# A transpose on one core: TensorE's program as a loop over three row chunks, PSUM in two halves, and copies that cover several ranges

## The chip, the core and the metric

The kernel runs on one core of a Trainium2 chip. The metric is the time on the device in microseconds (us) of one execution. The time before is 1265.63 us, the median of 8 runs (1265.09 to 1266.03).

## What is computed

```python
def setup_inputs():
    return {"x": np.random.randn(8192, 8192).astype(np.float32)}

def reference(x):
    return np.transpose(x)
```

The input and the output are float32, 268.44 MB each. The input is read once from HBM, and the output is written once.

## The kernel before

The input has 8192 rows and 8192 columns. The work is cut into 128 chunks: two halves of 4096 columns (`s`), each with 64 groups of 128 rows (`c`), first all of `s` = 0, then all of `s` = 1. The list `chunks` holds them in this order, and the loop over `t` (from 0 to 127) is written out in full when the program is made: every engine gets straight code, with no loop in it.

For each chunk one DMA loads 128 rows x 4096 columns (2 MB, 16 KB on each of 128 partitions) into one of three input buffers `ins[t % 3]` (line 99). TensorE turns the chunk in 32 transposes of 128 x 128 (line 139). Each transpose takes every fourth column of a block of 512 columns, so four transposes (`b`) make one block `q`, and a chunk has eight blocks. A block goes into one of eight PSUM tensors of 128 x 512, one for each bank. Even blocks are copied out by ScalarE (line 150) and odd ones by VectorE (line 152), each with one copy of 128 x 512.

The copies go into nine region buffers of 16 KB on each partition. A region collects one block `q` over up to eight chunks, so that its store writes long rows: a full region holds 1024 output columns, and its store moves 2 MB. The dictionary `window` says which region a block is collecting in, since which chunk. The blocks are out of step with one another: in chunk `t` one block's region is complete and closes (`q` = `c` mod 8), and in the next chunk that block opens a new region, taken from the list `free`. At the seam, between `s` = 0 and `s` = 1, a region holds the last groups of the one half and the first of the other, and two smaller stores empty it. The regions at the very start and at the very end are smaller too. There are 128 loads and 142 stores.

What sets the order around the change:

- SP (SyncE) issues all DMAs, into one queue, in the order in which the code writes them. First come the loads of chunks 0 to 2. Then for each chunk `t` come the stores of the blocks that close in it (line 172 for the first store, line 28 for all others), each behind a wait for its copy, and after them the load of chunk `t` + 3 behind a wait for TensorE's last transpose of chunk `t`.
- Within a chunk TensorE takes the blocks in the order `(c + k) % 8`, so the block that closes comes first, and the block that opens a new region comes last. It waits for the load of the chunk and, for each block, for the copy that empties its bank.
- A copy waits for TensorE. The copy that opens a region also waits until all stores from that region have landed (the semaphore `s_st` of the region, line 127).

The program's source is printed with its line numbers here.

Of the kernel before, what the change touches and what calls it, by code (L numbers as in the profile page):

```python
# [24 lines left out]
def wide_dma(nc, eng, queue, out, in_):  # L25


    return eng.add_instruction(
        mybir.InstDMACopy(
            mode="Copy",  # L30
            name=nc.get_next_instruction_name(),
            engine=eng.engine,
            ins=[physical(in_)],
            outs=[physical(out)],
            queue=queue,
        )
    )


@with_exitstack  # L40
def kernel(
    ctx: ExitStack,
    tc: tile.TileContext,
    x: bass.AP,
    out: bass.AP,
):

    nc = tc.nc
    P = 128
    N, M = x.shape
    assert x.shape == out.shape[::-1]
    dt = x.dtype

    S = 32
    B = 4  # L60
    W = 8
    NR = S // B
    NIN = 3
    NREG = 9
    NPS = 8
    CH = N // P
    J = S * P

    with tc.tile_critical():  # L69
        nc.alloc_sbuf_tensor("pad", [P, 32], dt)  # L70
        ident = nc.alloc_sbuf_tensor("ident", [P, P], dt).ap()
        ins = [nc.alloc_sbuf_tensor(f"in{k}", [P, J], dt).ap() for k in range(NIN)]
        regs = [nc.alloc_sbuf_tensor(f"reg{k}", [P, B * W * P], dt).ap() for k in range(NREG)]
        pss = [nc.alloc_psum_tensor(f"ps{k}", [P, B * P], dt).ap() for k in range(NPS)]

        s_id = nc.alloc_semaphore("s_id")
        s_ld = [nc.alloc_semaphore(f"s_ld{k}") for k in range(NIN)]
        s_st = [nc.alloc_semaphore(f"s_st{k}") for k in range(NREG)]
        s_pe = nc.alloc_semaphore("s_pe")
        s_cp = [nc.alloc_semaphore("s_cpa"), nc.alloc_semaphore("s_cpv")]  # L80

        nc.gpsimd.memset(ident, 0.0).then_inc(s_id, 1)  # L82
        nc.gpsimd.wait_ge(s_id, 1)
        nc.gpsimd.affine_select(  # L84
            out=ident,
            in_=ident,
            compare_op=mybir.AluOpType.not_equal,
            fill=1.0,
            base=0,
            pattern=[[-1, P]],  # L90
            channel_multiplier=1,
        ).then_inc(s_id, 1)
        nc.tensor.wait_ge(s_id, 2)

        chunks = [(s, c) for s in range(M // J) for c in range(CH)]

        def load(t):
            s, c = chunks[t]
            nc.sync.dma_start(
                out=ins[t % NIN], in_=x[c * P:(c + 1) * P, s * J:(s + 1) * J]  # L100
            ).then_inc(s_ld[t % NIN], 16)

        for t in range(NIN):
            load(t)

        n = 0
        copied = [0, 0]
        bank = [None] * NPS
        free = list(range(NREG))
        stored = [0] * NREG  # L110
        window = {}
        stores = 0
        for t, (s, c) in enumerate(chunks):
            nc.tensor.wait_ge(s_ld[t % NIN], 16 * (t // NIN + 1))
            closing = []
            for q in [(c + k) % NR for k in range(NR)]:
                if q not in window:


                    span = (q - c) % W + 1  # L120
                    r = free.pop(0)
                    parts = [(s, c, min(c + span, CH))]
                    if c + span > CH and t + span < len(chunks):
                        parts.append((s + 1, 0, c + span - CH))
                    window[q] = (t, r, parts)
                    if stored[r]:
                        (nc.scalar, nc.vector)[q % 2].wait_ge(s_st[r], 16 * stored[r])
                t0, r, parts = window[q]
                k = [p[0] for p in parts].index(s)
                base = B * P * sum(z - a for _, a, z in parts[:k])  # L130
                _, a, z = parts[k]
                rows = (z - a) * P
                view = regs[r][:, base:base + B * rows].rearrange("p (b i) -> p b i", b=B)
                ps = pss[n % NPS]
                e = q % 2
                if bank[n % NPS] is not None:
                    nc.tensor.wait_ge(*bank[n % NPS])
                for b in range(B):
                    last = nc.tensor.transpose(  # L139
                        ps[:, b * P:(b + 1) * P],  # L140
                        ins[t % NIN][:, q * B * P + b:(q + 1) * B * P - B + b + 1:B],
                        ident,
                    )
                last.then_inc(s_pe, 1)
                n += 1
                o = view[:, :, (c - a) * P:(c - a + 1) * P]
                i = ps.rearrange("p (b i) -> p b i", b=B)
                (nc.scalar, nc.vector)[e].wait_ge(s_pe, n)  # L148
                if e == 0:
                    cp = nc.scalar.copy(out=o, in_=i)  # L150
                else:
                    cp = nc.vector.tensor_copy(out=o, in_=i)  # L152
                cp.then_inc(s_cp[e], 1)
                copied[e] += 1
                bank[(n - 1) % NPS] = (s_cp[e], copied[e])
                if t + 1 == t0 + sum(z - a for _, a, z in parts):
                    closing.append((q, e, copied[e]))
            for q, e, count in closing:
                t0, r, parts = window.pop(q)
                nc.sync.wait_ge(s_cp[e], count)  # L160
                base = 0
                for s_, a, z in parts:
                    rows = (z - a) * P
                    j0 = s_ * J + q * B * P
                    dst = out[j0:j0 + B * P, a * P:a * P + rows]
                    dst = dst.rearrange("(q b) i -> q b i", q=P)
                    src = regs[r][:, base:base + B * rows]
                    base += B * rows
                    if stores:
                        st = wide_dma(nc, nc.sync, "qSPDynamicHW", dst, src)  # L170
                    else:
                        st = nc.sync.dma_start(
                            out=dst, in_=src.rearrange("q (b i) -> q b i", b=B)
                        )
                    st.then_inc(s_st[r], 16)
                    stores += 1
                    stored[r] += 1
                free.append(r)
            if t + NIN < len(chunks):
                nc.sync.wait_ge(s_pe, n)  # L180
                load(t + NIN)
        for r in range(NREG):
            nc.sync.wait_ge(s_st[r], 16 * stored[r])

# [29 lines left out]
```

## Time and profile before

| what | value |
|---|---|
| median of 8 runs | 1265.63 us |
| the profiled execution | 1265.43 us |
| its span | 1263.7 us |
| TensorE matmul busy | 746.2 us (59%), 4096 instructions |
| TensorE weight load busy | 722.3 us (57%), 4096 instructions |
| VectorE busy | 354.1 us (28%), 512 instructions |
| ScalarE busy | 300.9 us (24%), 513 instructions |
| data that the DMA queues moved | 537.51 MB, mean 425 GB/s |
| a load, median from issue to landing | 23.6 us |
| a store of 2 MB, median from issue to landing | 22.6 us |

The span runs from the first to the last record of the program in one profiled execution; the execution's own time is 1.7 us longer. "Busy" is the time in which an engine works on an instruction, and waits are not in it. The profile also cuts the span into 40 equal slices and gives for each the busy share of the DMA engines in tenths and what they moved in GB/s. There are 16 DMA engines on the core, and each DMA's rows are spread over all of them. A DMA queue's row gives its packets, the bytes in MB and the time of its packets as a share of the 16 engines' span: q1 is the queue of the loads and stores, and the queues marked "instruction" bring the engines' own programs. In a group of instructions the line of the kernel and the engine come first, then busy time and the mean time of one in ns, then the idle time before the group and what ended most of it. PE is TensorE, PEld its weight loads, DVE VectorE, ACT ScalarE, and SPq the queue in which SP issues DMAs.

### The profile page before, as it was taken

To read this page: it belongs to the slowest core of one execution; us is meant where nothing else is said; L and a number is where in the kernel's file an instruction comes from. 1 tells how busy PE (TensorE), PEld (TensorE's weight loads), DVE (VectorE), ACT (ScalarE), POOL (GpSimd) and SP (SyncE) were. 2 spreads that over 40 slices of the span, in tenths; PEclk is the share of its full clock that TensorE was granted. 3 is DMA by queue.
4 is the path that set the end of the run, shared out by engine and by line. 5 is a ranking of instruction groups with operands and counts; after the bars stand their busy time and mean duration, and the time that the engine had idled before them with its cause. 6 is when DMAs were issued, how large, how long until landed. Compare 5 with 4: busy or idle time off the path is not lost.

```text
span 1263.7 us, 9807 instructions
## 1 busy us (share of the span) xinstructions
PE 746.2 (59%) x4096; PEld 722.3 (57%) x4096; DVE 354.1 (28%) x512; ACT 300.9 (24%) x513; POOL 0.7 (0%) x6
## 2 busy tenths in 40 slices
PE   6656656565566655656556656666566665656561
PEld 6655556564566555655555655665556655656561
DVE  3322322322223222232222322223222232232220
ACT  3322222222222222222222222222222222222220
POOL 0000000000000000000000000000000000000000
PEclk9887786868767777676886786767777778686865
DMA  9999999999999999999999999999999999999998
GB/s 379 430 428 428 429 430 426 430 430 428 429 428 429 429 427 430 430 429 428 429 425 415 430 429 428 429 429 429 428 428 430 429 428 429 429 429 429 429 427 353
DMA packets 39308, 537.51 MB, mean 425 GB/s; under 512 B 4320, under 2 KB 4832, under 8 KB 6240
## 3 DMA queue, kind: packets, MB, share of 16 engines
q1 hardware_dynamic: 39264, 536.89, 99.9%
q8 instruction: 32, 0.52, 0.2%
q14 instruction: 12, 0.10, 0.0%
HBM read 268.44 MB, written 268.44 MB: 425 GB/s over the span
## 4 chain that ended last, share of the span: by engine, by line
DMA 78%; PE 19%; issue 0%; ACT 0%; SPq 0%; ACTq 0%
DMA in<-in_x_dram 78%; PE ps L139 19%; ACT reg L150 0%; SPq L209 0%; ACTq L148 0%; SPq L69 0%
## 5 line engine op out<-in xcount | busy, mean ns | idle before, releaser
L139 PE MATMUL ps<-ident,in 128*128 128x128 f32 x4096 | 746.2, 365 | 490.5 <-DMA in<-in_x_dram 490.5
L139 PEld LDWEIGHTS ps<-ident,in 128*128 128x128 f32 x4096 | 722.3, 220 | 514.2 <-DMA in<-in_x_dram 505.7
L152 DVE COPY reg<-ps 128x512 f32<-128x512 f32 x512 | 354.1, 692 | 882.8 <-PE ps L139 881.4
L150 ACT COPY reg<-ps 128x512 f32<-128x512 f32 x512 | 299.6, 585 | 935.6 <-PE ps L139 932.9
L150 ACT ACT_TABLE_LOAD x1 | 1.3, 1283 | 0.9 <-SPq L69 0.9
L84 POOL TENSOR_SCALAR_AFFINE_SELECT ident<-ident 128x128 f32<-128x128 f32 x1 | 0.3, 292 | 0.2 <-POOL ident L82 0.2
L82 POOL MEMSET ident<- 128x128 f32 x1 | 0.2, 204 | 0.5 <-SPq L69 0.5
L198 POOL MEMSET const-bfloat16-1.0<- 128x1 bf16 x1 | 0.1, 101 | 0.0
L198 POOL MEMSET const-uint8-127<- 128x1 uint8 x1 | 0.1, 101 | 0.0
L198 POOL MEMSET const-float32-0.0<- 128x1 f32 x1 | 0.1, 98 | 0.2 <-issue 0.2
L198 POOL MEMSET const-float32-1.0<- 128x1 f32 x1 | 0.1, 98 | 0.0
## 6 DMA issues: line engine op xcount, KB each, us to landing
in<-in_x_dram SPq DMA_DIRECT2D x128, 2048.0 KB, 23.6
out_dram<-reg SPq DMA_DIRECT2D x114, 2048.0 KB, 22.6
out_dram<-reg SPq DMA_DIRECT2D x4, 1792.0 KB, 19.8
out_dram<-reg SPq DMA_DIRECT2D x4, 1536.0 KB, 19.8
out_dram<-reg SPq DMA_DIRECT2D x4, 1280.0 KB, 19.6
out_dram<-reg SPq DMA_DIRECT2D x4, 1024.0 KB, 19.5
out_dram<-reg SPq DMA_DIRECT2D x4, 768.0 KB, 18.1
out_dram<-reg SPq DMA_DIRECT2D x4, 512.0 KB, 16.5
```

Of the source, the lines that this page charges most:

```text
L82: nc.gpsimd.memset(ident, 0.0).then_inc(s_id, 1)
L84: nc.gpsimd.affine_select(out=ident, in_=ident, compare_op=mybir.AluOpType.not_equal, fill=1.0, base=0, pattern=[[-1, P]], channel_multipl ...
L139: last = nc.tensor.transpose(ps[:, b * P:(b + 1) * P], ins[t % NIN][:, q * B * P + b:(q + 1) * B * P - B + b + 1:B], ident,)
L150: cp = nc.scalar.copy(out=o, in_=i)
L152: cp = nc.vector.tensor_copy(out=o, in_=i)
L198: nc = _bacc.Bacc("TRN2", target_bir_lowering=False, num_devices=1)
```

## The change

The changed kernel moves the same data in the same DMAs, with the same chunks, the same regions and the same buffers for the input. Five things are different.

1. **TensorE's program is a loop.** The function `transposes(t)` writes out one chunk. Chunks 0 and 1 are written out; the other 126 are 42 turns of a hardware loop with three chunks in it (one for each input buffer). A loop can't wait for rising counts, so TensorE takes back what it waited for: it waits until a load's semaphore is 16 and subtracts 16, and it waits until a half of PSUM is free (`s_bank`) and subtracts 1.
2. **PSUM is in two halves.** Each half is one tensor of 128 x 2048 and holds four blocks. TensorE always takes blocks 0 to 3 into the first half and 4 to 7 into the second, and signals after 16 transposes instead of after 4. ScalarE empties the first half, VectorE the second.
3. **One copy for several blocks.** All regions are one tensor `regs`. Where the places of neighbouring blocks in it lie a fixed distance apart and have the same row length, one copy takes up to four blocks. Where a block of the half closes, the four are cut into at least two copies, and the one with the closing block goes first.
4. **The wait for a region's earlier store** stands ahead of all copies of the half in which a region opens.
5. **The order on SP**: in each chunk the load of chunk `t` + 3 comes first and the stores after it. Among the stores of one chunk, the region that was opened first goes first.

The core of the diff (`SIZE` is the elements of a region on a partition, `NH` is 4, `T` is 128):

```diff
-        regs = [nc.alloc_sbuf_tensor(f"reg{k}", [P, B * W * P], dt).ap() for k in range(NREG)]
-        pss = [nc.alloc_psum_tensor(f"ps{k}", [P, B * P], dt).ap() for k in range(NPS)]
+        regs = nc.alloc_sbuf_tensor("regs", [P, NREG * B * W * P], dt).ap()
+        pss = [nc.alloc_psum_tensor(f"ps{h}", [P, NH * B * P], dt).ap() for h in range(2)]
...
+        def transposes(t):
+            k = t % NIN
+            nc.tensor.sem_inc(s_ld[k], -16).wait_op(s_ld[k], 16, "sem-ge")
+            for h in range(2):
+                if t:
+                    nc.tensor.sem_inc(s_bank[h], -1).wait_op(s_bank[h], 1, "sem-ge")
+                for b in range(NH * B):
+                    j = (h * NH + b // B) * B * P + b % B
+                    tr = nc.tensor.transpose(
+                        pss[h][:, b * P:(b + 1) * P],
+                        ins[k][:, j:j + B * P - B + 1:B],
+                        ident,
+                    )
+                tr.then_inc(s_pe, 1)
+
+        T = len(chunks)
+        nc.tensor.wait_ge(s_id, 2)
+        for t in range(T % NIN):
+            transposes(t)
+        with nc.Fori(0, T // NIN, engines=[nc.tensor.engine]):
+            for t in range(NIN):
+                transposes(T % NIN + t)
...
-            for q in [(c + k) % NR for k in range(NR)]:
...
-                (nc.scalar, nc.vector)[e].wait_ge(s_pe, n)
...
+            for h in range(2):
+                eng = (nc.scalar, nc.vector)[h]
...
+                        if stored[r]:
+                            eng.wait_ge(s_st[r], 16 * stored[r])
...
+                ends = [closes(window[h * NH + g], t) for g in range(NH)]
+                if any(ends) and len(runs) == 1:
+                    runs = [runs[0][:NH // 2], runs[0][NH // 2:]]
+                runs.sort(key=lambda u: not any(ends[g] for g in u))
+                eng.wait_ge(s_pe, 2 * t + h + 1)
+                for u in runs:
+                    off, dist = place[u[0]]
+                    dims = [list(regs.ap[0]), [dist, B], [1, P]]
+                    if len(u) > 1:
+                        dims.insert(1, [place[u[1]][0] - off, len(u)])
+                    o = bass.AP(regs.tensor, regs.offset + off, dims)
...
+                    if any(ends[g] for g in u):
+                        cp.then_inc(s_cp[h], 1)
...
+                        if u is runs[-1]:
+                            eng.wait_ge(s_cp[h], copied[h])
+                            eng.sem_inc(s_bank[h], 1)
+                    elif u is runs[-1]:
+                        cp.then_inc(s_bank[h], 1)
+            if t + NIN < T:
+                nc.sync.wait_ge(s_pe, 2 * t + 2)
+                load(t + NIN)
+            closing.sort(key=lambda k: window[k[0]][0])
...
-            if t + NIN < len(chunks):
-                nc.sync.wait_ge(s_pe, n)
-                load(t + NIN)
```

## The prediction, made before the changed kernel ran

> **What bounds the kernel now.** I read the page first, from the DMA rows up.
>
> ```profile
> DMA  9999999999999999999999999999999999999998
> GB/s 379 430 428 428 429 430 426 430 430 428 429 428 429 429 427 430 430 429 428 429 425 415 430 429 428 429 429 429 428 428 430 429 428 429 429 429 429 429 427 353
> ...
> q1 hardware_dynamic: 39264, 536.89, 99.9%
> q8 instruction: 32, 0.52, 0.2%
> q14 instruction: 12, 0.10, 0.0%
> ...
> L139 PE MATMUL ps<-ident,in 128*128 128x128 f32 x4096 | 746.2, 365 | 490.5 <-DMA in<-in_x_dram 490.5
> L139 PEld LDWEIGHTS ps<-ident,in 128*128 128x128 f32 x4096 | 722.3, 220 | 514.2 <-DMA in<-in_x_dram 505.7
> L152 DVE COPY reg<-ps 128x512 f32<-128x512 f32 x512 | 354.1, 692 | 882.8 <-PE ps L139 881.4
> L150 ACT COPY reg<-ps 128x512 f32<-128x512 f32 x512 | 299.6, 585 | 935.6 <-PE ps L139 932.9
> ```
>
> All 16 DMA engines are busy in every slice, at about 429 GB/s. TensorE is busy 59% of the span, VectorE 28%, ScalarE 24%, and each idles for the one before it. The queue alone bounds the kernel: 536.87 MB at 429 GB/s are 1251.4 us of the span of 1263.7. The change moves no byte of q1, so only the other 12.3 us can be won, and anything on the engines is free until a transfer is issued late. The two low slices are the start (first packet after 2 us, slow first packets) and the end (353 GB/s). The end is what I looked into.
>
> Each DMA reports its landing 16 times in the trace, once for each DMA engine. I took, for some loads and the last store, the 16 landing times, sorted, in us behind the first of the 16:
>
> ```
> load 0    0 .02 .02 .05 .08 .14 .16 .25 .26 .29 .30 .31 .33 .44 .48 .54
> load 30   0 .06 .19 .28 .30 .39 .56 .93 1.01 1.67 1.71 1.83 1.83 2.22 2.75 3.03
> load 63   0 .06 .29 .55 .86 1.04 1.07 1.92 3.01 3.05 3.21 3.22 3.31 3.69 4.25 4.42
> load 126  0 .11 .42 .66 1.45 2.42 2.66 4.13 6.27 6.44 6.50 6.69 6.78 7.11 7.39 7.46
> ```
>
> The engines drift apart, in steps. A step of 1.3 to 1.6 us (3.03 to 4.42, 2.22 to 3.69) follows each of the 32 fetches of q8, and always on one engine. Those 16 KB fetches come after every 248 to 266 TensorE instructions (16 KB / 256 = 64 B each): they load TensorE's own program. Eight engines end 6.3 to 7.5 us behind and the other eight 0 to 4.1: 32 fetches in turn on eight engines are four each, 4 x 1.45 = 5.8 us. The 12 fetches of q14 (8 KB; by the instruction counts ScalarE 5, VectorE 5, SyncE 2) make smaller steps, up to 1 us. Every DMA has its rows split over the engines in a fixed way, so no engine takes work from a late one, and the kernel ends with the latest.
>
> **Step 1: TensorE's loop (no fetches).** 42 turns over three chunks leave 128 + 192 of 8192 transpose instructions in the program. A turn is 96 x 2 + 9 semaphore instructions + 2 for the loop = 203, some 13 KB, less than one fetched block. If it stays in the engine, the eight lose four steps: 7.5 - 5.8 = 1.7 us behind at most. Then the other eight are the latest, at 4.13. No row shows a backward branch, so I bound its price: none to three blocks fetched a turn. Three is the case in which the body lies across a block boundary (the first crossing comes after some 220 to 240 of the instructions that the trace shows; the body takes places 138 to 341, so it does) and only two blocks are held: the first block again, the second again, and the one after it ahead of need. I take none, because the q8 fetches go round eight engines before they repeat, which looks to me like eight places for blocks, of which the loop uses two. That is an inference, not a row.
>
> [...]
>
> **Step 2: fewer copies.** The changed program holds 264 ScalarE and 259 VectorE copies instead of 512 each; with the semaphore instructions 330 and 324 instead of 577 and 576. At 128 instructions to 8 KB that is three fetches each instead of five: 12 become 8. The latest of the non-TensorE engines was hit by about three of the 12; it loses none to two steps of 1 us: 4.1 becomes 2.1 to 4.1, middle 3.1. Sum of steps 1 and 2: 7.5 - 3.1 = 4.4 us earlier (3.3 to 5.4). The copies themselves: four at 692 ns are 2.8 us at most for a half, inside a chunk's 9.76 us (three loads land 29.28 us apart). That a merged one is cheaper gains nothing, since both engines wait over 880 us for TensorE.
>
> **Step 3: the order on SP, and the store wait.** Now:
>
> ```profile
> SPq L99 <- PE ps L139: 465.9, 125, 8.8
> SPq L28 <- DVE reg L152: 321.2, 63, 9.3
> SPq L28 <- ACT reg L150: 311.1, 64, 9.1
> ...
> ACT reg L150 <- DMA out_dram<-reg: 2.7, 2, 1.4
> ...
> DVE reg L152 <- DMA out_dram<-reg: 1.5, 2, 1.0
> ```
>
> Today store t goes ahead of load t+3, and the new region's copy is the last of its chunk, so the wait for the store before costs four short waits in all. Afterwards load t+3 goes ahead of store t, and the wait for the region (nine regions, so that of store t-1 in chunk t+1) stands before a whole half. The queue then holds load t+1, store t-2, load t+2, store t-1: three transfers of 4.88 us, so the half that opens a region is copied 14.6 us after its load landed, not at once. Behind that wait stand that engine's copies of chunk t+1; behind them store t+1, TensorE's next write of the half (chunk t+2), and with it load t+5 on SP. A new wait, then, of some 8 to 10 us in most chunks. What hides it: between the landing of store t-1 and the place of load t+5 in the queue lie four transfers (load t+3, store t, load t+4, store t+1), 19.5 us; the chain needs 2.8 (copies) + up to 6.6 (a chunk's 32 transposes) + 1.0 (issue to first packet, from load 0) = 10.4. Cover of 9 us is left, more than a fast engine's lead of 7.5 us. I cost it at nothing; with the cover gone each us would be paid in up to 128 chunks.
>
> **Step 4: the two ends.**
>
> ```profile
> 1212.50 41.05 SPq L28 DMA_DIRECT2D out_dram<-reg  x10
> ...
> 1230.13 6.58 PE L139 MATMUL ps<-ident,in 128*128 128x128 f32 x32 [3.39 <-DMA in<-in_x_dram]
> ...
> 1236.28 0.69 DVE L152 COPY reg<-ps 128x512 f32<-128x512 f32 x1 [0.87 <-PE ps L139]
> 1236.81 0.58 ACT L150 COPY reg<-ps 128x512 f32<-128x512 f32 x1 [0.65 <-PE ps L139]
> ```
>
> Here all last stores stand ready while the queue is full. After the change: load 127 lands at 0; stores 124, 125, 126 end at 4.9, 9.8, 14.6. VectorE's half of chunk 126 waits for store 124 (4.9), is copied at 4.9 + 4 x 0.69 = 7.7; TensorE's half of chunk 127 ends at 7.7 + 3.3 = 11.0, past store 125; four copies end at 13.8, and the first of the last eight stores has a packet at 14.8. The queue ran out at 14.6. Gap 0.2 us; bounds 0 and, with a half of TensorE late, 3.6. I take 0.5. At the start loads 0 to 2 cover the 15 us in which the first halves are copied, as now: nothing.
>
> **Sum.** -4.4 + 0.5 = -3.9 us. The profiled execution took 1265.43 us (1.7 more than its span), 0.2 under the median of 1265.63 of the eight runs: 1265.4 - 3.9 = **1261.5 us**, alone 1259 to 1264 (-5.4, and one us for the stretch near 685 us where all engines lose 0.9 with no cause I can name; -3.3 + 2 at the other end).
>
> **Rivals.**
> - *The loop fetches itself again.* Place: the backward branch. Price: each fetch 1.45/8 = 0.18 us on the latest engines. One block a turn: 42 - 32 = +10 fetches, +1.8 us, 1267. Two: 84, +9.4, 1275. Three: 126, +17, 1282. It decides from one block a turn on. For it: the body crosses a boundary, and a fetch today comes at each crossing and never more than one. Against it: the eight places.
> - *The stalls make TensorE the bound.* Three chunks have 29.28 us, TensorE needs 3 x 6.5 = 19.5; it decides if a turn stalls for over 9.8 us. At 12 us: +2 x 42 = 90 us, 1350. Against it: a fetch packet takes 1.0 us.
> - *The change does nothing to the end.* The skew goes, but the wait of step 3 or the gap at the end gives it back, or the q14 engines stay as late as 6 us: 1263.5 to 1267.
>
> **How the numbers follow.** Forecast 0.57; fetching again 0.25 (0.06 at one block, 0.07 at two, 0.12 at three); no effect 0.11; TensorE bound 0.07. The range runs from 1259 to 1276: three blocks and the stalls (0.19) stay outside it. 0.2%, 2.5 us, is about what a measurement of this kernel can tell from no change. Of the forecast 0.50 lies below 1263.1 and 0.07 within; within 0.2% are further 0.07 of no effect and 0.04 of one block: faster 0.50, same 0.18, slower 0.32.
>
> **What would show it.** Step 1: q8 with a handful of packets instead of 32, and the last landings within 4 us of each other instead of 6 to 7; with 40, 80 or 130 packets the first rival holds. Step 2: eight packets on q14. Step 3: ScalarE and VectorE waiting for out_dram landings in most chunks, and slices still at 429. Step 4: the last slice. I am wrong if slices in the middle fall below 425, which would mean that loads are issued too late.

## The result, and the profile after

The changed kernel takes 1270.39 us (median of 11 runs, 1267.58 to 1273.87), the kernel before 1265.68 beside it (31 runs, 1265.09 to 1266.20). The ratio on record is 1.0041, with a 95% interval of 1.0034 to 1.0049 (the two medians alone give 1.0037): slower by 4.7 us, where 1261.5 was forecast. The time lies inside the range of 1259 to 1276. The profiled execution of the changed kernel took 1269.2 us, 3.8 more than that of before and 1.2 under its own median. Four of the 11 runs took 1273.2 to 1273.9 us, and no trace shows what these lost.

The page after, with the rows that answer to those of before:

```profile
DMA  9999999999999999999999999999999999999988
GB/s 385 426 428 430 429 428 429 429 429 430 430 429 429 430 430 429 429 430 430 430 425 413 430 430 430 430 429 429 429 430 429 429 430 429 430 430 424 427 341 366
...
q1 hardware_dynamic: 39264, 536.89, 99.8%
q14 instruction: 8, 0.07, 0.0%
q8 instruction: 1, 0.02, 0.0%
...
L117 PE MATMUL ps<-ident,in 128*128 128x128 f32 x4096 | 726.9, 357 | 512.4 <-PEq L114 503.7
L197 DVE COPY regs<-ps 128x512 f32<-128x512 f32 (+3 forms) x259 | 301.8, 1207 | 940.1 <-DMA out_dram<-regs 471.6
L197 ACT COPY regs<-ps 128x512 f32<-128x512 f32 (+3 forms) x264 | 247.2, 992 | 984.4 <-DMA out_dram<-regs 659.3
```

The fetches went as forecast: q8 has one packet instead of 32, q14 eight instead of 12. In the middle the slices still stand at 429 to 430 (425 and 413 are the dip near 685 us, which before has as well, and 424 stands near 1150 us), so the queue did not run dry there. New are the releasers: both copying engines now idle longest for a landing of a store (out_dram<-regs), and TensorE for the freeing of a half of PSUM (line 114). The slices of 341 and 366 in place of 427 and 353 are the end.

The waits after, first those of the engines, then those of the queue in which SP issues DMAs (us in total, times, longest us):

```profile
ACT regs L197 <- DMA out_dram<-regs: 659.3, 63, 20.4
...
PE ps L117 <- PEq L114: 503.7, 137, 6.6
DVE regs L197 <- DMA out_dram<-regs: 471.6, 60, 10.0
```

```profile
SPq L103 <- PE ps L117: 764.8, 125, 11.4
SPq L28 <- DVE regs L197: 217.7, 64, 11.1
SPq L28 <- ACT regs L197: 132.8, 47, 5.1
```

The wait of step 3 comes 123 times, 60 to 63 on each engine, 7.9 us on VectorE and 10.5 us on ScalarE in the mean; before it came four times. The load now waits 765 us for TensorE in place of 466, the stores 350 in place of 632, and the queue still holds enough to stay full.

So the page alone does not tell where 3.8 us went. The landings do. For the same loads as in the prediction, the 16 landing times in us behind the first:

```
load 30    0 .02 .03 .05 .07 .11 .13 .28 .29 .34 .43  .60 1.18 2.17 2.89 3.27
load 63    0 .01 .03 .04 .10 .12 .13 .27 .28 .34 .43  .60 1.44 2.89 3.27 4.95
load 126   0 .01 .05 .08 .10 .18 .20 .36 .40 .59 .82 3.00 3.70 3.87 4.26 9.53
```

The steps of the fetches are gone: at load 126 eleven engines land within 0.8 us, where eight were 6.3 to 7.5 behind. But one engine is now 9.5 us behind. Apart from one step of 0.9 us at load 97, beside the q14 fetch at 937.0 us, it did not get there in steps: its distance is 3.5, 4.7, 5.7, 7.6 and 9.5 us at loads 40, 60, 78, 100 and 126, some 0.07 us in each chunk, while the second latest stays at 3.3 to 4.3.

In absolute times, load 126 landed on the latest engine at 1220.3 us before and at 1218.5 after. It now stands one store (4.9 us) earlier in the queue, so on equal terms the latest engine is 1218.5 - (1220.3 - 4.9) = 3.1 us later, and the second latest 2.2 us earlier (1213.2 against 1215.4). The remaining 0.7 us come at the end. The timeline of the end of the changed kernel (start us, us, engine, line, and in brackets the idle time before it with its releaser):

```profile
1233.40 2.42 DVE L197 COPY regs<-ps 128x1024 f32<-128x1024 f32 x3 [7.44 <-DMA out_dram<-regs]
...
1235.97 3.29 PE L117 MATMUL ps<-ident,in 128*128 128x128 f32 x16 [4.30 <-PEq L114]
1239.37 2.48 DVE L197 COPY regs<-ps 128x512 f32<-128x512 f32 x4 [3.54 <-PE ps L117]
```

This is the chain of step 4: store 124 lands on the latest engine at 1233.4, then VectorE's half of chunk 126, TensorE's last half, its copies, and the last stores. Most of the 16 engines stand idle meanwhile (in the three stretches of 2 us from 1230 on the DMAs move 131, 37 and 147 GB/s; one engine's share of 429 is 27), but the late one loses by it no more than the 0.7 us.

### The profile page after: what moved, and what is told of

Its sections match the earlier page's. It is cut to its first block, busy times and chain, and to the rows that moved or that the text cites. A ratio compares the mean times of both kernels' runs of the same rounds, so it can differ in the third digit from the quotient of the medians.

```text
span 1267.4 us, 9647 instructions
## 1 busy us (share of the span) xinstructions
PE 726.9 (57%) x4096; PEld 700.4 (55%) x4096; DVE 301.8 (24%) x259; ACT 248.5 (20%) x265; POOL 0.7 (0%) x6
## 5 line engine op out<-in xcount | busy, mean ns | idle before, releaser
L117 PE MATMUL ps<-ident,in 128*128 128x128 f32 x4096 | 726.9, 357 | 512.4 <-PEq L114 503.7
L117 PEld LDWEIGHTS ps<-ident,in 128*128 128x128 f32 x4096 | 700.4, 219 | 538.4 <-issue 538.1
L197 DVE COPY regs<-ps 128x512 f32<-128x512 f32 (+3 forms) x259 | 301.8, 1207 | 940.1 <-DMA out_dram<-regs 471.6
L197 ACT COPY regs<-ps 128x512 f32<-128x512 f32 (+3 forms) x264 | 247.2, 992 | 984.4 <-DMA out_dram<-regs 659.3
```

The lines of the kernel that those rows point to most:

```text
L117: tr = nc.tensor.transpose(pss[h][:, b * P:(b + 1) * P], ins[k][:, j:j + B * P - B + 1:B], ident,)
L197: cp = nc.scalar.copy(out=o, in_=i) if h == 0 else nc.vector.tensor_copy(out=o, in_=i)
```

## The experiments

Theories. The first one: step 3 costs the time, by the order on SP, by the wait ahead of a half, or by both. Its rivals: the loop itself, the halves with the merged copies, or the end. When the middle turned out to lose the time with a full queue, a second question was added: whether the engines' own work slows the DMA engines (coupling).

For each kernel the table has the median, its ratio to the kernel before run beside it, the distance of the latest engine from the first at loads 30, 60, 100 and 126 (that of the second latest at 126 in brackets), and the gap at the end. This gap is the time from the latest landing of load 126 to the last landing, less the 46.9 us (load first) or 42.0 us (stores first) that it takes with DMAs alone. Distances and gaps come from the one profiled execution. The kernel before took 1265.68 to 1266.15 beside the different rows, so medians of two rows compare to some 0.5 us.

```
kernel                        median   ratio [95%]              30   60  100  126        gap
before                       1265.68                           3.0  4.4  7.5  7.5 (7.4)  0.0
after                        1270.39  1.0041 [1.0034, 1.0049]  3.3  4.7  7.6  9.5 (4.3)  0.8
e1  after, straight code     1268.35  1.0017 [1.0008, 1.0026]  3.3  4.6  7.5  7.9 (6.6)  0.8
e2  after, stores first      1264.45  0.9986 [0.9977, 0.9995]  3.6  3.6  5.4  5.4 (5.3)  1.5
e3  after, other last order  1268.88  1.0023 [1.0010, 1.0037]  3.6  6.0 10.2  9.5 (2.7)  0.2
e4  after, wait late         1265.37  0.9996 [0.9987, 1.0005]  3.5  3.5  5.9  6.8 (4.4)  0.1
e5  load first to chunk 111  1270.57  1.0039 [1.0025, 1.0053]  3.3  5.0  7.6  6.1 (2.5)  1.5
e6  load first from 112      1264.25  0.9984 [0.9975, 0.9993]  3.8  3.8  5.4  6.3 (6.1)  1.1
e7  three repairs            1264.03  0.9985 [0.9976, 0.9994]  3.3  3.3  4.8  6.1 (4.6)  0.1
e8  e2, straight code        1268.13  1.0015 [1.0006, 1.0025]  3.1  4.5  7.5  8.9 (7.5)  0.1
e10 before, load first       1266.01  1.0000 [0.9991, 1.0009]  3.2  4.6  7.7  7.8 (7.7)  0.0
e11 DMAs alone, load first   1264.13  0.9986 [0.9976, 0.9995]  3.3  3.0  4.8  4.8 (4.3)  0.0
e12 DMAs alone, stores first 1264.38  0.9985 [0.9975, 0.9994]  3.2  3.3  5.8  5.8 (5.8)  0.0
e13 e11 + loop, transposes   1269.66  1.0032 [1.0019, 1.0046]  4.6  9.6 10.6 10.6 (4.6)  0.0
e14 e12 + loop, transposes   1269.80  1.0028 [1.0017, 1.0039]  5.0  9.8 11.9 12.5 (4.1)  0.0
e15 e13, straight code       1266.51  1.0002 [0.9992, 1.0011]  5.1  6.9  7.8  7.8 (6.8)  0.0
e16 e13, wide matmuls        1264.07  0.9982 [0.9972, 0.9991]  3.5  3.4  5.5  5.5 (5.4)  0.0
e17 e11 + loop on VectorE    1264.06  0.9983 [0.9974, 0.9993]  3.3  3.2  4.5  4.5 (4.3)  0.0
e18 e13, loop of 24          1269.80  1.0029 [1.0018, 1.0041]  3.4  9.9 11.0 11.0 (4.4)  0.0
e19 after without copies     1263.47  0.9981 [0.9972, 0.9991]  3.6  3.6  6.2  6.2 (4.6)  0.0
```

### Which part of the change

**e1_unrolled**: the loop is undone, all else stays.

```diff
-        for t in range(T % NIN):
+        for t in range(T):
             transposes(t)
-        with nc.Fori(0, T // NIN, engines=[nc.tensor.engine]):
-            for t in range(NIN):
-                transposes(T % NIN + t)
```

> The changed kernel with TensorE's program written out again for all 128 chunks; everything else as changed. Theory 1 (lock): the loop did what was forecast, 32 fetches are gone; the loss comes from the new order on SP and the store wait, which tie TensorE's work to the latest DMA engine. Then the fetches come back on q8 (about 32), eight engines get their 5.8 us back, and the time stays at 1270 or rises to about 1275 if the one late engine is among the eight. Theory 2 (loop): the late engine, which fell behind by 0.07 us a chunk in the changed kernel, is slowed by something that the looped program does; then the steady growth is gone and the time is that of before, 1265 to 1267. Theory 3 (end): the loss is the gap before the last eight stores; then 1270 to 1274 with the fetches.

q8 has 33 packets again, and the steps are back: the second latest engine goes from 4.3 to 6.6 us. The time falls all the same, by 2.0 us, because the latest engine goes from 9.5 to 7.9; it lies between the ranges of theory 2 (1265 to 1267) and theory 1 (1270 or more). The steady growth is not gone with the loop. One engine can be followed through the sorted landings, and it falls back as fast as in after, from a start that is 1.0 us lower (us behind the first engine):

```
load     40   50   60   66   78   88   96   124
after  3.49 4.15 4.71 5.17 5.72 6.30 6.71  9.37
e1     2.46 3.11 3.76 4.17 5.26 5.98 6.42  8.65
```

Up to load 88 the fetches of e1 keep another engine further behind than this one (4.6 us at load 60, where this one has 3.76). At load 126 the two latest engines of e1 stand at 7.9 and 6.6 us: here the lag by fetches and the lag of the one engine don't add. Why it starts lower, no run tells.

**e2_store_first**: SP's old order, stores ahead of the load; loop, halves and merged copies stay.

```diff
-            if t + NIN < T:
-                nc.sync.wait_ge(s_pe, 2 * t + 2)
-                load(t + NIN)
             closing.sort(key=lambda k: window[k[0]][0])
...
                 free.append(r)
+            if t + NIN < T:
+                nc.sync.wait_ge(s_pe, 2 * t + 2)
+                load(t + NIN)
```

> The changed kernel with SP's order of before: in each chunk the stores first, then the load of chunk t+3. Theory 1: the waits for out_dram landings on ScalarE and VectorE (659 and 472 us in the changed kernel) fall under 100 us each, the late engine stays within 4 us, and the time is 1260.5 to 1262, 4 us under the kernel before. Theory 2: the late engine stays late, 1268 to 1271. Theory 3: the last stores are ready earlier too, because the wait ahead of them is one transfer instead of three: 1261 to 1264, which does not tell it from theory 1.

5.9 us less than after, and 1.5 less than before: the loss hangs on the order. The slow growth is gone from the latest engine (3.6 at loads 30 and 60, 5.4 at 100 and 126); another one still moves, by 0.01 us a load (3.40 at load 100, 3.70 at 124). Three points of the expectation failed: the time lies above the ranges of theories 1 and 3, the latest engine is 5.4 us behind and not within 4, and ScalarE's waits did not fall. The waits of this kernel:

```profile
DVE regs L197 <- PE ps L117: 935.5, 128, 14.1
...
ACT regs L197 <- PE ps L117: 498.1, 68, 10.0
ACT regs L197 <- DMA out_dram<-regs: 486.4, 60, 9.4
```

ScalarE still waits 486 us for stores, and nothing is lost by it. What differs is who waits for ScalarE. The same stretch of the timeline, first of after, then of e2:

```profile
730.72 1.99 ACT L197 COPY regs<-ps 128x512 f32<-128x512 f32 x3 [7.82 <-DMA out_dram<-regs]
731.33 0.55 SPq L28 DMA_DIRECT2D out_dram<-regs  x1
...
732.86 6.36 PE L117 MATMUL ps<-ident,in 128*128 128x128 f32 x32 [3.64 <-PEq L114]
```

```profile
725.26 1.99 ACT L197 COPY regs<-ps 128x512 f32<-128x512 f32 x3 [7.76 <-DMA out_dram<-regs]
...
730.35 6.32 PE L117 MATMUL ps<-ident,in 128*128 128x128 f32 x32 [3.64 <-PEq L114]
```

In after, TensorE starts 0.15 us behind ScalarE's last copy (730.72 + 1.99 = 732.71), and these copies start with the landing of a store on the latest DMA engine. In e2 the copies are done at 727.25, 3.1 us before TensorE starts, so the store does not release it.

**e10_before_load_first**: the kernel before, with only the load moved ahead of the stores.

```diff
+            if t + NIN < len(chunks):
+                nc.sync.wait_ge(s_pe, n)
+                load(t + NIN)
             for q, e, count in closing:
...
-            if t + NIN < len(chunks):
-                nc.sync.wait_ge(s_pe, n)
-                load(t + NIN)
```

> The kernel before with one part of the change alone: in each chunk the load of chunk t+3 goes ahead of the stores on SP. TensorE's code stays straight, copies stay single. If the load-first order costs by itself (through the later landing of the store that a region waits for, or through the queue), it costs here what it cost in the changed kernel, 4 to 6 us: 1270 to 1272. If it costs only together with halves and merged copies, because there the wait stands ahead of a whole half, the time is 1265 to 1267.

No difference from before (1266.01 against 1266.01), although both engines now wait 536 to 537 us for stores. So with straight code and single copies neither the order nor such a wait shows in the time. A slow drift could hide here: fetches put the latest engine at 7.8 us, and another moves by 0.03 us a load (2.48 at load 100, 3.17 at 124). TensorE is hardly held: it waits 419 us in all for loads and 43 us for copies. A stretch of its timeline:

```profile
726.27 6.61 PE L139 MATMUL ps<-ident,in 128*128 128x128 f32 x32 [3.32 <-DMA in<-in_x_dram]
...
731.22 2.54 ACT L150 COPY reg<-ps 128x512 f32<-128x512 f32 x5 [8.69 <-DMA out_dram<-reg]
```

Here a wait holds the block that opens, which comes last, and the next chunk's blocks behind it; TensorE still starts with the landing of a load.

**e4_late_wait**: the block that opens a region gets a copy of its own, the last of its half, and only this copy waits for the region's store.

```diff
                         if stored[r]:
-                            eng.wait_ge(s_st[r], 16 * stored[r])
+                            opening[q - h * NH] = (s_st[r], 16 * stored[r])
...
-                    if runs:
+                    if runs and g not in opening and runs[-1][-1] not in opening:
...
-                runs.sort(key=lambda u: not any(ends[g] for g in u))
+                runs.sort(key=lambda u: (u[0] in opening, not any(ends[g] for g in u)))
...
                 for u in runs:
+                    if u[0] in opening:
+                        eng.wait_ge(*opening[u[0]])
```

> The changed kernel, load first on SP as changed, but the block that opens a region is copied last in its half by a copy of its own, and only that copy waits for the region's earlier store. Theory 1: the half's bank still comes free only after the store of t-1 has landed, three transfers after the load, so TensorE's work stays tied to the latest engine; 1268 to 1271, the growth of 0.07 us a chunk stays. A rival to it (the wait ahead of the whole half is what costs): 1261 to 1264.

1265.37, between the two expectations and nearer to the rival's: with the load still first, putting the wait behind three blocks wins 5.0 us against after. The latest engine still moves away, but less (0.03 us a load from load 100 to 124, where after has 0.07). So after's loss takes the order and the place of the wait together.

**e8_store_first_unrolled**: e2 with straight code for TensorE (the two edits of e1 and e2 together).

> Stores first on SP, and TensorE's program written out, so that its 32 fetches are back. Against stores first with the loop (1264.45) it gives what the loop is worth by itself. By the prediction's step 1 the fetches put eight engines 5.8 us back, so the latest goes from 5.4 to 7 or 8 us behind: 1266.5 to 1268. If the fetches cost nothing: 1264 to 1265.

1268.13 (0.1 above the range expected) against 1264.45 of e2: with the stores first **the loop alone is worth 3.7 us**. With the load first it costs 2.0 (after against e1). Against before, e8 measures the halves and merged copies in straight code: 2.1 us slower. Its profile has no gap at the end; its latest engine is 8.9 us behind in place of 7.5, and it was 7.5 up to load 125. The last step, of 1.4 us, falls together with a fetch of q8 at 1214.9 us (16 KB, 1.03 us), the 33rd; before has 32, and q14 fetches nothing between 1208.6 and 1230.1 us. So 1.4 of the 1.9 us between the two profiled executions (1267.34 and 1265.43) look like one more block of TensorE's program, met by an engine that was already the latest, and not like a cost of the copies. Whether that is the whole 2.1 us was not isolated.

### Where in the run

**e5_load_first_middle** and **e6_load_first_end**: the load first up to chunk 111 and the stores first from 112 on, and the reverse.

```diff
-            if t + NIN < T:
+            if t + NIN < T and (t < 112):
...
+            if t + NIN < T and not (t < 112):
+                nc.sync.wait_ge(s_pe, 2 * t + 2)
+                load(t + NIN)
```

> The changed kernel, load first on SP up to chunk 111, stores first (as before the change) from chunk 112 on. Stores first throughout took the changed kernel from 1270.4 to 1264.45 us; this run and the next say where. If the loss of the load-first order is made in the middle (one DMA engine falls back by 0.07 us a chunk while TensorE's work hangs on a store's landing), the engine is 9 us late here too and the time is 1268 to 1270. If it is made at the end (the last eight stores are issued too late, behind a store's landing, a copy, half a chunk of TensorE and a copy), the time is 1264 to 1266.

> The reverse: stores first up to chunk 111, load first from 112 on. Loss in the middle: the late engine has 5 to 6 us at the end and the time is 1264 to 1266. Loss at the end: 1268 to 1270.

e6 has the new order only at the end and stays at 1264.25, like e2; e5 has it in the middle and takes 1270.57, 0.6 above the range expected. The loss is in the middle, where e5's latest engine falls back as that of after does (5.0 at load 60, 8.7 at load 110). The size of e5's loss is partly its own: at the switch its slices fall to 412 and 408, and the latest engine goes from 8.7 us behind at load 110 to 6.1 at 126, as if the early ones waited for it there.

**e3_tail_order**: in the last chunk ScalarE's stores go ahead of VectorE's.

```diff
-            closing.sort(key=lambda k: window[k[0]][0])
+            closing.sort(key=lambda k: (k[1] if t == T - 1 else 0, window[k[0]][0]))
```

> The changed kernel with one thing different: in the last chunk the four stores of ScalarE's half are issued before the four of VectorE's, so that the queue has 22 MB/4 = 5.8 MB of work while VectorE waits. Theory 3: the gap of 6.5 us of a slice (341 GB/s instead of 429) closes and the time falls by 3 to 5 us, to 1265 to 1267. Theory 1: the late engine has no gap there (its last stores follow one another), so it falls by under 1 us: 1269 to 1270.

Not settled by the times: 1268.88 with runs from 1266.85 to 1278.72, and the profiled execution is the longest (1278.72), with time lost on all engines in the middle. In it the gap at the end is 0.2 us in place of 0.8, so some 0.6 us is what this order could win.

### The queue alone, and with one engine beside it

**e11_dma_load_first** and **e12_dma_store_first**: all DMAs in the order of after (or with stores first), no transposes, no copies; the regions hold zeros.

```diff
+        for r in range(NREG):
+            nc.vector.memset(regs[:, r * SIZE:(r + 1) * SIZE], 0.0).then_inc(s_ms, 1)
...
+            nc.sync.wait_ge(s_ld[t % NIN], 16 * (t // NIN + 1))
             if t + NIN < T:
-                nc.sync.wait_ge(s_pe, 2 * t + 2)
                 load(t + NIN)
...
-                nc.sync.wait_ge(s_cp[h], count)
+                nc.sync.wait_ge(s_ms, r + 1)
```

> Only the DMAs of the changed kernel in its order (load of t+3, then stores of t), both released by the landing of load t. TensorE's transposes and all copies are left out, and the regions hold zeros, so the output is zeros. No TensorE program, so no fetches. If the queue alone makes one engine fall back in this order, the last load's landings are spread over 5 to 10 us and the time is 1264 to 1270. If it takes the coupling with TensorE and the copies, the spread stays under 2 us, and the time is 1255 to 1258.

> The same with the stores of t ahead of the load of t+3; transposes and copies are left out and the output is zeros. Against the run with the load first it gives what the order is worth to the queue alone: nothing (within 1 us), if the coupling is the cause; 4 to 6 us less, if the order in the queue is.

1264.13 and 1264.38, only 1.6 to 1.9 us less than the kernel before beside them (1266.01), and no difference that can be told by the order. The queue without any engine's work is not the faster queue that coupling called for. The page of e11:

```profile
GB/s 386 427 423 422 429 429 428 426 430 429 429 429 430 429 430 428 430 430 429 429 421 408 430 430 429 430 430 431 429 429 430 429 430 429 430 430 429 430 430 355
...
q1 hardware_dynamic: 39264, 536.89, 100.1%
q14 instruction: 2, 0.02, 0.0%
```

Without any program of TensorE to fetch the latest engine still ends 4.8 us behind, the slices near 685 us dip as ever (421, 408), and the last slice is 355. This is about the floor for these DMAs.

**e13_dma_load_first_pe** adds a loop of 42 turns of 96 transposes of the identity to e11, which waits for nothing; **e14_dma_store_first_pe** does so with e12.

```diff
+        with nc.Fori(0, T // NIN, engines=[nc.tensor.engine]):
+            for b in range(NIN * NR * B):
+                nc.tensor.transpose(pss[b // 16 % 2][:, b % 16 * P:(b % 16 + 1) * P], ident, ident)
```

> The DMAs alone, load first, and TensorE at work beside them without any wait: 42 turns of 96 transposes of the identity, tied to no DMA, busy for the first 700 to 800 us. Copies are left out, and the output is zeros. If TensorE's activity as such stretches one engine's store packets, the spread of a load's landings grows while TensorE works (0.07 us a chunk, 5 us in all) and stops growing after it. If it takes the coupling, the spread stays as without TensorE.

> The DMAs alone with the stores first, and TensorE's free loop of transposes beside them (443 us); copies left out, output zeros. If the order in the queue matters for how TensorE hurts one engine, the spread stays near 5.8 us and the time at 1264.4; if it doesn't, 1269 to 1270 as with the load first.

1269.66 and 1269.80: the loop alone, tied to no transfer, makes the DMAs 5.4 to 5.5 us longer, in either order. The page of e13:

```profile
PE 441.7 (35%) x4032; PEld 441.4 (35%) x4032; DVE 31.2 (2%) x9; POOL 0.7 (0%) x6
...
PE   9999999999999900000000000000000000000000
...
GB/s 386 426 426 429 428 429 428 429 429 430 428 429 428 429 429 430 429 430 430 428 420 417 428 430 430 430 430 430 429 430 428 430 429 430 430 430 429 430 430 278
```

TensorE is busy in the first 14 slices, to about 443 us. In that time the latest engine goes from 3.4 us behind (load 20) to about 9.5; from load 60 on, when TensorE is silent, it moves by 1.0 us in 66 loads, half of it at the dip near 685 us and half beside a q14 fetch at 929.6 us. The second latest stays at 3.4 until then. The slices don't show it while it happens (426 to 430 from the second to the 14th): by an estimate from these numbers, 6.1 us in 443 on one engine of 16 take 0.4 GB/s from the 429. The bill comes in the last slice, 278 in place of 355.

**e15 to e18** take this apart: e15 writes the same transposes out in straight code, e16 has 12 matmuls of 128 x 512 in a turn in place of 96 transposes, e17 has a loop of copies on VectorE and nothing on TensorE, e18 has 168 turns of 24 transposes.

```diff
-        with nc.Fori(0, T // NIN, engines=[nc.tensor.engine]):
+        for t in range(T // NIN):
```

```diff
-            for b in range(NIN * NR * B):
-                nc.tensor.transpose(pss[b // 16 % 2][:, b % 16 * P:(b % 16 + 1) * P], ident, ident)
+            for b in range(12):
+                nc.tensor.matmul(
...
+                    regs[:, :512],
```

```diff
+        with nc.Fori(0, T // NIN, engines=[nc.vector.engine]):
+            for b in range(4):
+                nc.vector.tensor_copy(out=pss[b % 2], in_=regs[:, :NH * B * P]).then_inc(s_d, 1)
```

```diff
-        with nc.Fori(0, T // NIN, engines=[nc.tensor.engine]):
-            for b in range(NIN * NR * B):
+        with nc.Fori(0, 4 * (T // NIN), engines=[nc.tensor.engine]):
+            for b in range(NIN * NR * B // 4):
```

> The DMAs alone, load first, and the same 4032 free transposes as straight code; copies left out, output zeros. About 31 fetches come in the first 440 us and put eight engines back by 5 to 6 us. If the loop is what hurts the one engine, no engine is over 8 to 9 us late and the time is 1266 to 1268. If TensorE's work is, one engine is 10 us late or more, 1269 to 1273.

> The DMAs alone, load first, and TensorE free in a loop of 42 x 12 matmuls of 128 x 128 by 128 x 512, a fourth of the instructions per us or fewer for like data; copies left out, output zeros. If the stream of instructions hurts, the spread stays at 5 us and the time at 1264 to 1265. If reading SBUF or writing PSUM does, the late engine falls back while TensorE works, 1267 to 1270.

> The DMAs alone, load first, and VectorE free in a loop of 168 copies of 128 x 2048 from SBUF to PSUM, for some 400 us; TensorE does nothing, output zeros. If any engine's work beside the queue puts one DMA engine back, 1266 to 1270; if it is TensorE's alone, 1264 to 1265.

> The DMAs alone, load first, and the same 4032 free transposes in 168 turns of 24 instead of 42 of 96; copies left out, output zeros. A turn is 50 instructions and stays well inside one block. If a turn's size (its nearness to the next block) is what hurts, 1264 to 1265 and no packet on q8; if the looped stream of small instructions is, 1269 to 1271.

Wide matmuls (435 us busy, on a zeroed region) and VectorE's copies (386 us) cost nothing: 1264.07 and 1264.06. The short loop costs as much as the long one (1269.80). Straight code costs 2.4 us, with 31 packets on q8, and what part of it is theirs was not isolated; there the second latest engine is at 6.8. In straight code, too, one engine can be followed through the sorted landings, and it falls back as fast as in the loops, hidden behind others that fetches have put at 5 to 6.6 us (us behind the first engine):

```
load               20   24   28   32   33
e15 straight     1.73 2.39 3.11 3.67 3.83
e18 loop of 24   1.75 2.34 3.04 3.72 3.90
e13 loop of 96   2.98 3.66 4.30 4.95 5.12
```

That is 0.16 us a load in all three. In e15 this engine stands at 6.9 when TensorE falls silent and stays there (6.90 at load 48, 6.88 at 60). So it does not take a loop: beside these 4032 transposes one engine falls back, looped or straight. In e13 it stands at 9.6 then: it was 1.2 us further behind at load 20, and loads 41 and 43 brought 0.8 to 0.9 us each, with no fetch beside them. These two steps are not explained. A slower drift exists without such work: in e12 one engine goes from 1.03 at load 20 to 2.62 at load 40, and stands still then. What it is in the small instructions was not isolated: e16 has not only wider matmuls, but a fourth of the matmuls and of the weight loads (1008 each in the trace against 4032), and the profile records a fourth as many; whether the recording has a part in the drift, no run tells.

**e19_no_copies**: after without copies, and so without the waits for PSUM and for regions; the same loop, the same transposes from the loaded chunks, the load first; the regions hold zeros.

```diff
-                if t:
-                    nc.tensor.sem_inc(s_bank[h], -1).wait_op(s_bank[h], 1, "sem-ge")
...
+            nc.sync.wait_ge(s_pe, 2 * t + 2)
             if t + NIN < T:
-                nc.sync.wait_ge(s_pe, 2 * t + 2)
                 load(t + NIN)
```

> The changed kernel, load first and with its loop of three chunks, but without copies, without the wait for a half of PSUM and without the wait for a region's store; the output is zeros. TensorE is released by the load's landing alone, load t+3 and the stores of t by TensorE's last transpose of t. If it is the region wait that puts TensorE's work where it hurts, the late engine stays at 5 to 6 us and the time is 1264 to 1265.5. If load first with the loop is enough, 1269 to 1271.

1263.47, the least of all and 0.5 under the range expected. Its loop runs as long as that of e2 (741.8 against 743.8 us busy) and its order is that of after, but TensorE is released by loads, and the latest engine stands still from load 78 to 126 (6.2). It also lacks the copies, so it doesn't alone prove that the release matters; e17 speaks against the copies as a cause.

### A version that is better than both

**e7_three_repairs**: loop, halves and merged copies of after, with the edits of e2, e4 and e3 together.

> Stores first on SP, the opening block copied last with the wait for its region ahead of it alone, and in the last chunk ScalarE's four stores ahead of VectorE's four. Loop, halves of PSUM and merged copies as changed. Stores first alone gives 1264.45 us, with an idle queue of 6 us at the end (25 to 180 GB/s at 1232 to 1238 us), of which the latest engine, 5.4 us behind, feels about 1.6. If that gap is what is left, it closes: 1260.5 to 1263. If the latest engine alone sets the end: 1263 to 1264.5.

1264.03, against before 0.9985 [0.9976, 0.9994]. Its waits:

```profile
ACT regs L200 <- PE ps L117: 982.2, 128, 9.8
DVE regs L200 <- PE ps L117: 934.2, 128, 14.3
...
ACT regs L200 <- DMA out_dram<-regs: 0.9, 3, 0.5
```

Hardly any wait for a store is left, and no gap at the end (0.1 us). It stands at the floor of e11 and e12, inside the second range expected: the latest engine alone sets the end. One engine falls back here as well, by 0.05 us a load (1.07 at load 40, 4.84 at 100, 5.95 at 124), but it is the latest only from load 100 on.

## Why the prediction was wrong

Taken in one order, the runs give the change as halves and merged copies +2.1 (e8 against before), the loop -3.7 (e2 against e8), load first with the wait ahead of a half +5.9 (after against e2). That this makes +4.3, with +4.7 measured, is no check, since the three differences join end to end. Taken in the other order, load first is worth +0.2 (e1 against e8) and the loop +2.0 (after against e1). The parts don't add one by one, because the latest of 16 engines sets the end (in 14 rows of the table the last landing follows its landing of load 126 by the time that DMAs alone take, with a gap of 0.0 to 0.1 us): in straight code fetches already hold engines some 7.5 us behind at load 100 (before, e1 and e8), and the one that falls back, at 6.71 in e1 at load 96, passes them late.

- **Step 1, the loop: right about the fetches, -3.7 in size with the stores first, +2.0 with the load first.** It does not fetch itself again: q8 has one packet in 42 turns, at 30.5 us, inside the first turn (between its second chunk and its third), which fits a body across a block boundary, and none in the other 41. How many blocks TensorE holds no run shows: the eight places of the prediction, and the two of its dearest case, were its author's suppositions. The first two rivals had a chance of 0.32 together and are dead. Steps 1 and 2 together were put at -4.4; the floor left less to win.
- **Step 2: the count was right (8 packets), the worth was not seen.** The copies were costed at nothing and the halves not at all. Beside stores first and straight code the two came to 2.1 us; in the profiled execution 1.4 us of lag came with a 33rd block of TensorE's program, which the loop does not fetch.
- **The floor was missing.** That the latest engine would be 3.1 us behind took nearly all lag for fetches. With no program of TensorE it is 4.8 to 5.8 us behind, and DMAs alone take 1264.1. A forecast of 1261.5 lay below what these DMAs can do; the best that could come out was a gain of some 2 us.
- **Step 3 is the step that failed.** It said: "I cost it at nothing", with a cover of 9 us. The wait came as forecast (8 to 10 us in most chunks), and the cover held: the slices stayed full, and the sign that the prediction gave for being wrong, slices in the middle under 425, came in one slice alone outside the dip that before has too (424). The reasoning asked only whether a transfer is issued late. The cost came by a path that it did not look at: with this order and wait one DMA engine falls back by 0.07 us in each chunk, from 3.5 to 9.5 us, looped (after) or not (e1). In the looped program 5.9 us hang on it. The cause is shown in so far as undoing the order (e2), moving the wait (e4) or releasing TensorE by loads alone (e19) removes most or all of it, and as transposes without any tie set one engine back too, looped or straight (e13, e14, e15, e18). That the wait acts by setting when TensorE works is argued, not shown.
- **Step 4: 0.5 forecast, 0.8 measured** on the profiled execution, inside its bounds. The rest of the low end slices is paid by engines that are early.
- **The third rival** named the place ("the wait of step 3 gives it back"), but by a gap in the queue, and its 1263.5 to 1267 was too little.

How the engine falls back can be seen in its packets, in part. A packet of 16 KB takes 611 ns; 635 packets of after took 617 to 659 ns, 171 of before, 301 of e2 and 785 of e1. The trace doesn't name the engine of a packet. But in chunks 78 to 117 of after all of the 149 lengthened packets start in the time in which the latest engine is on a store, which is half of the time, if this time is taken from landing to landing, and 136 if it is taken 1.4 us earlier. Their excess is 2.4 to 2.7 us; the engine falls back by 3.4 us meanwhile, 0.9 of them the step at load 97. In before 1 to 3 of 70 start there.

Open is why. Whether it hangs on TensorE's work during these store phases can't be read off: taken 1.4 us ahead of the landings, TensorE works in 170 of 200 us of them in after and in 129 of 198 in e2; taken from landing to landing, in 124 and in 186. Order and wait change the rate, but not in one direction (loads 100 to 124: 0.07 us a load in after, 0.05 in e7 with stores first and no wait, 0.03 in e4, 0.01 in e2); by what, no run tells. Straight code lengthens as many packets (375 in e15, 381 in e13). Why it is one engine, and stores rather than loads, stays open too. A tenth region, which might take the wait away and leave the order, was not tried.

## What to carry to other kernels

Where a DMA queue bounds a kernel, measure its DMAs alone first: here that gives 1264.1 us, where the kernel before takes 1266.0 beside it, and the best version with all its work (e7) 1264.0. Then read the landings by DMA engine, since here the latest of 16 set the end (9.5 us behind at load 126 and 1270.39 us in after, 5.4 and 1264.45 in e2). Lags of different engines did not add, and a cut in one lag showed only down to the next: the loop took the fetches away, and was worth 3.7 us with the stores first and -2.0 with the load first. An engine that fell back slowly stayed hidden behind others (in e1 up to load 88), so follow each of the 16, and not the latest alone, before a cause is named. A wait that held no transfer up was not free in the looped program: moving it won 5.0 us (e4), undoing the order on SP 5.9 (e2), and no slice of after shows this before the last two. In e10, with straight code and single copies, 536 to 537 us of such waits on each copying engine cost nothing (1266.01 against 1266.01).

## What the runs showed of the hardware

- Transposes of 128 x 128 that wait for nothing (4032 of them, 442 us busy) set one DMA engine of 16 back by 0.16 to 0.17 us in each load while they run, in loops of 24 or 96 and in straight code alike. Looped, the end comes 5.5 us later (1269.66 against 1264.13), in straight code 2.4 (1266.51). Matmuls of 128 x 512 (435 us busy) and VectorE's copies (386 us) don't move the end (1264.07, 1264.06).
- A TensorE loop of 203 instructions in a turn ran 42 turns with one instruction packet of 16 KB, in the first turn, where straight code takes 32 (before) or 33 (e1, e8). With the stores first the loop is 3.7 us faster (1264.45 against 1268.13), with the load first 2.0 slower (1270.39 against 1268.35).
- With TensorE and ScalarE silent and VectorE busy for 31 us only (e11, e12), the 16 DMA engines drift apart by 4.8 to 5.8 us up to load 126, in runs of 1264 us. Every kernel, these too, has two low slices near 685 us (421 and 408 in e11). No run explains them.
